# The first modulation vectors as VectorE sums, x^T last in halves, and the expert biases in one 128-partition tile

## The chip, the cores and the metric

The kernel runs on one core of a Trainium2 chip. The metric is the device time of one execution in microseconds (us), lower is better. Engines: PE does matmuls, DVE is VectorE, ACT is ScalarE, POOL is GpSimd, and SP here only issues DMAs. ACT issues DMAs of its own as well.

## The reference

One decoder layer on x (256 tokens by 1024) and a conditioning vector c (1024):

```python
mod = jax.nn.silu(c) @ w_ada + b_ada                  # 1024 x 6144
sh_a, sc_a, g_a, sh_f, sc_f, g_f = jnp.split(mod, 6)
h = x * (1.0 + sc_a) + sh_a
mix = hybrid_mixer(h, w_in, ret_norm_g, w_out, rel_bias)
x = layer_norm(DN_ALPHA * x + (1.0 + g_a) * mix, ln1_g, ln1_b)
h = x * (1.0 + sc_f) + sh_f
ff = moe(h, w_router, b_router, w_gate_up, b_gate_up, w_down, b_down)
x = layer_norm(DN_ALPHA * x + (1.0 + g_f) * ff, ln2_g, ln2_b)
```

The mixer multiplies h by w_in, feeds a top-64 sparse softmax attention with a relative bias and a retention branch, and projects the two with w_out. The mixture of experts picks 4 of 32 experts per token; each has 8 MB of gate and up weights, 4 MB of down weights, and bias rows b_gate_up and b_down.

## The kernel before, in words

Weights come on SP's queue as tiles of 128 x 2048 f32 (1 MiB) into a ring of six buffers (`rtile`, tag w); large named buffers (`spare`, tags x0 to x10) hold the rest. ACT's queue (`small`) carries small loads. A scheduler sets each engine's order from the dependences and its own cost estimates; `tc.issue_after` pins a few instructions behind others. Each engine executes its list strictly in order, and a DMA stands in the list of the engine that issues it, so a DMA that waits holds up what is behind it.

**Start.** `mod_step(0, k)` (L163, k = 0 to 7) loads eight tiles of w_ada, 128 input rows by the 2048 columns of sh_a and sc_a. PE multiplies each with silu(c) (cT, broadcast to 32 columns) into `pm` (L110 is the line of every matmul helper). xT, the transposed x, is loaded behind the sixth tile. Then follow in a row: copy of pm to SBUF (`modrow`, L172 on DVE and L173 on ACT), four PE transposes (`pmt`, L179), the sums with b_ada (`sc` L231, `sha` L232), and hh = xT * sc + sha in rounded fp32r, four blocks on ACT (L238) and four on DVE (L240). hl is what the rounding left (L243 to L245).

**Projections.** `split` cuts every weight tile into whi (ACT, L263) and wlo (DVE, or POOL for every fourth, L264). `proj_t` runs hh x whi, hl x whi and hh x wlo on PE. w_idx (544 columns) is the first tile projected, then twelve w_in tiles.

**Attention.** `softmax(s, r)`: POOL adds `bias` (a 1 MB tile of relative biases) to the scores (L415), PE makes logits pl, DVE adds (L420) and takes the maximum (L422), ACT exponentiates (L425), DVE takes reciprocals (L427) and scales (L429), PE transposes into pp (L433), ACT copies (L435). The last two calls, softmax(1,0) and softmax(1,2), run at 105 to 124 us; the value projection `pv` and the gate parts of the modulation stand among them on PE.

**Expert biases.** `bias_rows` loads b_gate_up three times over as 96 x 2048, b_down as 96 x 1024 (L510, ACT's queue), makes a bf16 copy (ACT, L512) and two correction terms (DVE, L514 and L515). raw_bias_gu takes the buffer of `bias` (tag nn) once POOL has read that for the last time.

**Experts.** Each expert's twelve 1 MiB tiles stream through the ring (SP, L775 and L783), PE multiplies them; the loads begin at 133 us, while the mixer still runs, as far as buffers are free.

Of the kernel before, what the change touches and what calls it, by code (L numbers as in the profile page):

```python
# [28 lines left out]
def layouts(inputs):  # L29
# [55 lines left out]
    dn = g["b_down"].reshape(2, 32, 512).transpose(1, 0, 2).reshape(32, 1024)  # L85
    out = {"head": head, "cst": cst, "hot": np.concatenate([hot, rel], 1),
# [7 lines left out]
def layer(ctx, tc, t, out):  # L94
# [41 lines left out]
    small(out=dec, in_=t["row"])  # L136
    ident_r = sb("ident_r", 128, 128, pool=keep, dt=F32R)
    V.tensor_copy(ident_r, ident)
    pick = sb("pick", 96, 32, pool=keep, dt=BF16)
    V.tensor_add(pick, ident[0:96, 0:32], ident[0:96, 32:64])  # L140
    V.tensor_add(pick, pick, ident[0:96, 64:96])
    ones = sb("ones", 128, 128, pool=keep)
    G.memset(ones, 1.0)
# [14 lines left out]
    def mod_step(part, k, w=None):  # L158
        if k == 0:
            mods[part] = ps("s", name="pm")  # L160
        pm = mods[part]
        w = rtile() if w is None else w
        load(out=w, in_=t["w_ada"][0, k * 128:(k + 1) * 128, part * 2048:(part + 1) * 2048])  # L163
        for j in range(4):
            mm(pm[32 * j:32 * j + 32], cT[:, k], w[:, j * 512:(j + 1) * 512], k == 0, k == 7)

    def mod_row(part):
        row = sb("modrow", 128, 512, pool=keep)
        if part:
            V.tensor_add(row, mods[part], b_ada[:, part - 1])  # L170
        else:
            V.tensor_copy(row[:, 0:256], mods[part][:, 0:256])  # L172
            first["mod"] = A.activation(row[:, 256:512], mods[part][:, 256:512], AF.Copy)  # L173
# [59 lines left out]
    sc1, sha = [v.rearrange("p a b -> p (a b)") for v in (sc1, sha)]
    hh = spare("hh", 0, F32R).rearrange("p (k t) -> p k t", k=8)
    hl = spare("hl", 1, F32R).rearrange("p (k t) -> p k t", k=8)
    for b in range(8):
        if b % 2 == 0:
            A.activation(hh[:, b], xT[:, b], AF.Identity, bias=sha[:, b:b + 1], scale=sc1[:, b:b + 1])  # L238
        else:
            first["h"] = V.tensor_scalar(hh[:, b], xT[:, b], sc1[:, b:b + 1], sha[:, b:b + 1], op0=OP.mult, op1=OP.add)  # L240
    for b in range(0, 8, 2):
        f2 = sb("hfull", 128, 2, 256, bufs=2, tag="zT")
        V.tensor_scalar(f2[:, 0], xT[:, b], sc1[:, b:b + 1], sha[:, b:b + 1], op0=OP.mult, op1=OP.add)  # L243
        A.activation(f2[:, 1], xT[:, b + 1], AF.Identity, bias=sha[:, b + 1:b + 2], scale=sc1[:, b + 1:b + 2])
        V.tensor_sub(hl[:, b:b + 2], f2, hh[:, b:b + 2].bitcast(F32))  # L245
# [8 lines left out]

    nsplit = [0]

    def split(w):
        i = nsplit[0]
        nsplit[0] += 1
        n = w.shape[1]  # L260
        hi = spare("whi", 2 + 2 * (i % 2), F32R)[:, 0:n]
        lo = spare("wlo", 3 + 2 * (i % 2), F32R)[:, 0:n]
        first["split"] = A.activation(hi, w, AF.Copy)  # L263
        (G if i % 4 == 3 and i < 13 else V).tensor_tensor(lo, w, hi.bitcast(F32), op=OP.subtract)  # L264
        return hi, lo
# [41 lines left out]
    w = rtile()[:, 0:544]  # L307
    load(out=w, in_=t["w_idx"])
    with tc.issue_after(first["mod"].ins), tc.issue_after(first["h"].ins):
        w = [d.rearrange("p (k c) -> p k c", k=8) for d in split(w)]  # L310
# [3 lines left out]
    with tc.issue_after(first["split"].ins):  # L314
        load_later()
# [10 lines left out]
    for b in range(2):  # L326
        A.activation(blocks(qiT[:, b]), back(pq[:, b]), AF.Copy)
# [180 lines left out]
    def bias_rows(name, n, **kw):  # L508
        raw = sb("raw_" + name, 96, n, 512, **kw)
        small(out=raw, in_=t[name].rearrange("p (h c) -> p h c", h=n))  # L510
        b = sb(name, 96, n, 512, pool=keep, dt=BF16)
        A.activation(b, raw, AF.Copy)  # L512
        for o in (64, 32):
            V.tensor_sub(raw[0:o], raw[0:o], b[0:o])  # L514
            V.tensor_copy(b[0:o], raw[0:o])  # L515
        return b
# [62 lines left out]
    split_wo(3)  # L579

# [566 lines left out]
```

## Time and profile before

| | |
|---|---|
| median of 3 runs | 1137.49 us (1134.46 to 1137.56) |
| profiled execution: time, span | 1137.54 us, 1135.9 us |
| mean granted clock of PE | 0.981 |
| busy: PE, DVE, ACT, POOL | 92%, 32%, 16%, 4% |
| moved from and to memory | 452 MB, mean 398 GB/s |
| chain that ended last, two largest parts | 57% DMA, 36% PE |

Busy shares are means over the span. The chain that ended last is followed back from the last instruction to whatever released it each time, so it says which resource the end hangs on. The stretches show the same per slice of time: PE's busy time, its granted clock (1.00 is 2.4 GHz, 0.50 is 1.2 GHz), and the rate of the DMAs.

### The profile page before, as it was taken

What the parts mean: (1) busy time and instruction counts of PE and PEld (TensorE: products, weight loads), DVE (VectorE), ACT (ScalarE), POOL (GpSimd) and SP (SyncE); (2) the same over time, 40 slices, a digit from 0 to 9 for tenths busy, and PEclk for the clock granted to TensorE, in tenths of its full rate; (3) what the DMA queues carried; (4) which work ended last, traced back from release to release, by engine and by line L of the source; (5) the groups of instructions that cost most, each with busy time, mean ns of one, the idle gap of its engine ahead of it and who ended that gap; (6) DMA issues with size and microseconds to landing.
All of it is one profiled execution on the core that took longest, in us unless ns stands there. A gap on an engine that the chain in (4) does not pass through costs nothing.

```text
span 1135.9 us, 12046 instructions
## 1 busy us (share of the span) xinstructions
PE 1044.3 (92%) x4939; PEld 440.9 (39%) x4939; DVE 360.4 (32%) x661; ACT 177.4 (16%) x292; POOL 49.4 (4%) x38
## 2 busy tenths in 40 slices
PE   7999999999999999999999899989988689999895
PEld 1776676344334333433333233323422233233232
DVE  0676786123122222221322122212221212212125
ACT  1534634101101000100110001000100001100001
POOL 0124110300000000000000000000000000000001
PEclk9899999999899999999999999999999889999998
DMA  9988995999999999999999999999999999999993
GB/s 381 364 320 303 382 385 226 369 421 421 420 422 420 422 420 422 420 422 421 422 421 420 421 421 422 421 422 420 421 421 421 421 419 421 421 421 421 421 416 139
DMA packets 65861, 451.99 MB, mean 398 GB/s; under 512 B 7380, under 2 KB 8573, under 8 KB 11817
## 3 DMA queue, kind: packets, MB, share of 16 engines
q1 hardware_dynamic: 63536, 447.52, 95.6%
q10 hardware_dynamic: 2266, 3.65, 1.0%
q8 instruction: 41, 0.67, 0.2%
q14 instruction: 18, 0.15, 0.0%
HBM read 450.05 MB, written 1.09 MB: 397 GB/s over the span
## 4 chain that ended last, share of the span: by engine, by line
DMA 57%; PE 36%; DVE 4%; ACT 1%; issue 1%; SPq 0%; ACTq 0%; DVEq 0%
DMA w<-in_w_gate_up 37%; DMA w<-in_w_down 19%; PE py L110 7%; PE pgate L110 7%; PE pup L110 6%; PE pm L110 3%; PE pr L110 2%; PE pv L110 2%; PE pz L110 2%; PE pg L110 1%; PE psc L110 1%; PE pb L110 1%; PE pq L110 1%; PE pact L879 1%; DVE wlo L264 1%
## 5 line engine op out<-in xcount | busy, mean ns | idle before, releaser
L110 PE MATMUL pgate<-w,xe 128*64 128x512 f32 x1024 | 341.4, 604 | 24.5 <-DMA w<-in_w_gate_up 24.4
L110 PE MATMUL pup<-w,xe 128*64 128x512 f32 x1024 | 347.4, 594 | 0.0
L110 PE MATMUL py<-w,aT 128*64 128x512 f32 (+1 forms) x1056 | 244.5, 592 | 10.2 <-DMA w<-in_w_down 8.4
L110 PEld LDWEIGHTS pup<-w,xe 128*64 128x64 f32 x1024 | 101.2, 137 | 148.5 <-issue 144.7
L110 PEld LDWEIGHTS pgate<-w,xe 128*64 128x64 f32 x1024 | 90.5, 136 | 173.4 <-issue 92.5
L851 DVE TENSOR_SCALAR sw_g<-pgate 128x512 f32<-128x512 f32 x32 | 22.1, 692 | 396.7 <-PE pgate L110 396.7
L110 PEld LDWEIGHTS py<-w,aT 128*64 128x64 f32 x1056 | 72.0, 137 | 134.3 <-issue 90.4
L897 DVE TENSOR_TENSOR y<-py,gf 64x512 f32<-64x512 f32 x62 | 42.7, 689 | 194.9 <-PE py L110 194.5
L852 ACT ACTIVATE act<-sw_g 128x512 f32<-128x512 f32 x32 | 20.1, 630 | 487.5 <-DVE sw_g L851 487.5
L924 DVE TENSOR_TENSOR acc<-acc,psc 128x512 f32<-128x512 f32 x60 | 38.6, 684 | 23.5 <-PE psc L110 23.5
L1076 POOL TENSOR_TENSOR acc<-acc,ln 128x512 f32<-128x512 f32 (+1 forms) x2 | 2.7, 1342 | 903.5 <-ACT acc L1075 903.5
L803 DVE TENSOR_SCALAR xe<-pg,ha,hb 128x128 f32<-128x128 f32 x64 | 25.7, 409 | 49.6 <-PE pg L110 36.4
L880 ACT ACTIVATE aT<-pact 128x512 f32<-128x512 f32 x32 | 19.1, 597 | 119.9 <-PE pact L879 119.9
L263 ACT ACTIVATE whi<-w 128x2048 fp32r<-128x2048 f32 (+1 forms) x17 | 31.3, 1840 | 34.9 <-DMA w<-lay_w_in 16.3
L804 ACT ACTIVATE xe<-pg,hb,ha 128x128 f32<-128x128 f32 x64 | 28.5, 457 | 47.6 <-DVE xe L803 47.6
L110 PE MATMUL pm<-w,cT 128*32 128x512 f32 x192 | 35.6, 677 | 0.0
L110 PE MATMUL psc<-yh,ohT 128*128 128x512 f32 x60 | 25.4, 464 | 10.9 <-ACT yh L911 7.8
L110 PE MATMUL pg<-oh,nh 128*128 128x256 f32 x128 | 34.8, 306 | 0.5 <-DVE oh L656 0.3
L911 ACT ACTIVATE yh<-y,gs 128x1024 fp32r<-128x1024 f32 x15 | 17.2, 1148 | 107.1 <-DVE y L897 107.1
L110 PEld LDWEIGHTS <-pick 96*64 96x64 bf16 x190 | 15.2, 109 | 47.0 <-issue 44.7
L110 PE MATMUL pg<-oh,nl 128*128 128x256 f32 x128 | 33.4, 293 | 0.0
L264 DVE TENSOR_TENSOR wlo<-w,whi 128x2048 fp32r<-128x2048 f32 (+1 forms) x14 | 30.4, 2172 | 6.4 <-ACT whi L263 6.4
(262 smaller groups left out, 857.1 us busy)
## 6 DMA issues: line engine op xcount, KB each, us to landing
w<-in_w_gate_up SPq DMA_DIRECT2D x256, 1024.0 KB, 19.8
w<-in_w_down SPq DMA_DIRECT2D x124, 1024.0 KB, 19.8
w<-in_w_ada SPq DMA_DIRECT2D x24, 1024.0 KB, 6.9
w<-lay_w_in SPq DMA_DIRECT2D x12, 1024.0 KB, 8.8
w<-lay_w_out SPq DMA_DIRECT2D x4, 1024.0 KB, 11.3
w<-in_w_down SPq DMA_DIRECT2D x7, 512.0 KB, 12.7
xT<-lay_xT SPq DMA_DIRECT2D x1, 1024.0 KB, 14.5
x<-in_x SPq DMA_DIRECT2D x2, 512.0 KB, 10.5
```

Of the source, the lines that this page charges most:

```text
L110: T.matmul(o, l, r, start=start, stop=stop)
L263: first["split"] = A.activation(hi, w, AF.Copy)
L264: (G if i % 4 == 3 and i < 13 else V).tensor_tensor(lo, w, hi.bitcast(F32), op=OP.subtract)
L803: return V.tensor_scalar(xes[h][:, i], src, ha[:, i:i + 1], hb[:, i:i + 1], op0=OP.mult, op1=OP.add)
L804: return A.activation(xes[h][:, i], src, AF.Identity, bias=hb[:, i:i + 1], scale=ha[:, i:i + 1])
L851: V.tensor_scalar(g, pg, 7.0, None, op0=OP.min)
L852: A.activation(s, g, AF.Sigmoid, scale=1.702)
L879: T.transpose(pa[:, 2 * i + j], act[:, 256 * i + j:256 * i + j + 255:2], ident)
L880: A.activation(aT, pa, AF.Copy)
L897: V.tensor_mul(y[o:o + CAP, c], py[64 * c:64 * c + 64], gf[64 * c:64 * c + 64, c * 512:(c + 1) * 512])
L911: A.activation(yh, y, AF.Copy, scale=gs)
L924: V.tensor_add(o, o, p_)
```

## The change

Four things are done.

1. c is loaded first, as a row; PE broadcasts it to all partitions with a row of ones (`pc`, L143), ACT takes silu into cB. The weights of sh_a and sc_a are laid out by output column (`ada_t`), and DVE multiplies each 128 x 1024 half tile by cB and sums it into one column of `mcol` (16 instructions, L168). PE's matmuls, the row copies and the transposes of this part are gone.
2. SP's order at the start is now c, six weight tiles, `row`, tiles 6 and 7 in halves with w_idx between, xT in two halves, then the w_in tiles. w_idx is split ahead of hh.
3. hl, cT, ident_r and pick are pinned behind hh; the copy f8 moves from DVE to ACT; the load of `bias` moves behind the copy of the indexer's queries (L355).
4. The expert biases become one 128 x 768 tile `btmp` in the buffer of `bias` (L539). DVE makes three bf16 parts (L541 casts, L543 subtractions), they are written to memory (L545) and read back as 96 x 3072 by three DMAs (L611).

```diff
+    crow = spare("crow", 5)[0:1, 0:1024]
+    load(out=crow, in_=t["c"])
...
+    cB = spare("cB", 4)[:, 0:1024]
+    for j in range(2):
+        pc = ps("s", name="pc")
+        pcs = T.matmul(pc, ones[0:1], crow[:, j * 512:(j + 1) * 512], start=True, stop=True)
+        cbs = A.activation(cB[:, j * 512:(j + 1) * 512], pc, AF.Silu)
...
+    def mod_sums(i, w, pieces=1):
+        n = 2048 // pieces
+        for p in range(pieces):
+            load(out=w[:, p * n:(p + 1) * n], in_=t["ada_t"][i, :, p * n:(p + 1) * n])
+        for b in range(2):
+            wb = w[:, b * 1024:(b + 1) * 1024]
+            first["sum"] = V.scalar_tensor_tensor(wb, wb, 1.0, cB, op0=OP.mult, op1=OP.mult,
+                                                  accum_out=mcol[:, 2 * i + b:2 * i + b + 1])
...
-        small(out=bias, in_=bass.AP(tensor=fap.tensor, offset=fap.offset, ap=[[1, 128], [384, H], [1, 256]]))
...
+    for i in range(8):
+        mod_sums(i, rtile() if i < 6 else spare("w", i - 6), 1 if i < 6 else 2)
+        if i == 0:
+            sums1 = first["sum"]
+        if i == 5:
+            load(out=dec, in_=t["row"])
+        if i == 6:
+            w_first = rtile()[:, 0:544]
+            load(out=w_first, in_=t["w_idx"])
+    for p in range(2):
+        load(out=xT[:, 4 * p:4 * p + 4], in_=t["xT"].rearrange("p (k t) -> p k t", k=8)[:, 4 * p:4 * p + 4])
...
-    for k in range(8):
-        mod_step(0, k, None if k < 6 else spare("w", k - 6))
-        if k == 5:
-            load(out=xT, in_=t["xT"].rearrange("p (k t) -> p k t", k=8))
-
-
-    ca = mod_cols(mod_row(0), 0, 4)
...
+    w_first = split(w_first)
+
+
+    sha, sc1 = sb("sha", 128, 8), sb("sc1", 128, 8)
+    V.scalar_tensor_tensor(sc1, mcol[:, 8:16], 1.0, b_sa[:, 8:16], op0=OP.add, op1=OP.add)
+    V.tensor_add(sha, mcol[:, 0:8], b_sa[:, 0:8])
...
+    with tc.issue_after(qis.ins):
+        small(out=bias, in_=bass.AP(tensor=fap.tensor, offset=fap.offset, ap=[[1, 128], [384, H], [1, 256]]))
...
-    b_gu = bias_rows("bias_gu", 4, pool=keep, tag="nn")
-    b_dn = bias_rows("bias_dn", 2, tag="k4a")
+    btmp = sb("btmp", 128, 2048, pool=keep, tag="nn")
+    raw, bpart = btmp[:, 0:768], btmp[:, 768:1920].bitcast(BF16).rearrange("p (o c) -> p o c", o=3)
+    small(out=raw, in_=t["biases"])
+    for o in range(3):
+        V.tensor_copy(bpart[:, o], raw)
+        if o < 2:
+            V.tensor_sub(raw, raw, bpart[:, o])
+    bd = dram.tile([3, 128, 768], BF16, name="bd")
+    small(out=bd.rearrange("o p c -> p o c"), in_=bpart)
+    b_all = sb("b_all", 96, 3072, pool=keep, dt=BF16)
...
+    with tc.issue_after(first["split"].ins):
+        for o in range(3):
+            small(out=b_all[32 * o:32 * o + 32].rearrange("r (u c) -> r u c", u=4),
+                  in_=bd[o].rearrange("(u r) c -> r u c", u=4))
```

The lines of the kernel shift with the change: L263 and L264 become L229 and L230, and the softmax's L415, L420, L422, L425, L427, L429, L433 and L435 become L443, L448, L450, L453, L455, L457, L461 and L463. Behind the names of the rows below stand `[waits ...]`: the engines or DMA lanes whose signal an instruction waits for.

The first place is DVE at the start. Before, the list up to hh was:

```order
L153 COPY cT<-sg 128x256
L172 COPY modrow<-pm 128x256
L231 SCALAR_TENSOR_TENSOR sc_177<-pmt,head 128x8
L232 TENSOR_TENSOR sha<-pmt,head 128x8
L240 TENSOR_SCALAR hh<-xT,sc_177,sha 128x256 x4
```

Now it begins with:

```order
L168 SCALAR_TENSOR_TENSOR w,mcol<-w,cB 128x1024 x8
L261 TENSOR_TENSOR sha<-mcol,head 128x8
L168 SCALAR_TENSOR_TENSOR w,mcol<-w,cB 128x1024 x6
L230 TENSOR_TENSOR wlo<-w,whi 128x544
L168 SCALAR_TENSOR_TENSOR w,mcol<-w,cB 128x1024 x2
L260 SCALAR_TENSOR_TENSOR sc_162<-mcol,head 128x8
L268 TENSOR_SCALAR hh<-xT,sc_162,sha 128x256 x4
```

The copy of the row and the sums with the transposed columns are replaced by sixteen products with sums, with the split of w_idx between the last of them.

The second place is ACT ahead of the exponentials (L425, now L453) of softmax(1,0). Before:

```order
L263 ACTIVATE whi<-w 128x2048 [waits DMAHW7_49,Pool_49]
L510 DMA raw_bias_dn<-lay_bias_dn 96x1024 [waits PE_49]
L425 ACTIVATE scr_69,sm<-scr_69,mx 128x256 [waits DVE_49,Activation_49]
L425 ACTIVATE scr_69,sm<-scr_69,mx 128x256
L425 ACTIVATE scr_69,sm<-scr_69,mx 128x256 [waits DVE_49,Activation_49]
L425 ACTIVATE scr_69,sm<-scr_69,mx 128x256
L263 ACTIVATE whi<-w 128x2048 [waits DMAHW2_49]
```

Now:

```order
L229 ACTIVATE whi<-w 128x2048 [waits DMAHW3_49,Pool_49]
L539 DMA btmp<-lay_biases 128x768 [waits DMAHW7_49,Pool_49]
L453 ACTIVATE scr_69,sm<-scr_69,mx 128x256 [waits DVE_49,Activation_49]
L453 ACTIVATE scr_69,sm<-scr_69,mx 128x256
L453 ACTIVATE scr_69,sm<-scr_69,mx 128x256 [waits DVE_49,Activation_49]
L453 ACTIVATE scr_69,sm<-scr_69,mx 128x256
L463 ACTIVATE scr_71<-pp 128x2x256 [waits PE_49]
```

The load of btmp, which waits for POOL's last read of `bias`, stands ahead of the exponentials; before, the load that waited for POOL (raw_bias_gu) stood behind them and behind the copies of pp, and the one here waited for PE.

The third place is DVE in softmax(1,0), whose scaling (L429, now L457) PE's transposes pp wait for. Before:

```order
L420 SCALAR_TENSOR_TENSOR scr_69<-pl,scr_69 128x512 [waits DVE_49,PE_49] x2
L422 TENSOR_REDUCE mx<-scr_69 128x2 [waits DVE_49] x2
L427 RECIPROCAL sm<-sm 128x2 [waits Activation_49]
L429 TENSOR_SCALAR scr_69<-scr_69,sm 128x256 [waits DVE_49]
L429 TENSOR_SCALAR scr_69<-scr_69,sm 128x256
L427 RECIPROCAL sm<-sm 128x2 [waits Activation_49]
L429 TENSOR_SCALAR scr_69<-scr_69,sm 128x256 [waits DVE_49]
L429 TENSOR_SCALAR scr_69<-scr_69,sm 128x256
```

Now:

```order
L448 SCALAR_TENSOR_TENSOR scr_69<-pl,scr_69 128x512 [waits DVE_49,PE_49] x2
L450 TENSOR_REDUCE mx<-scr_69 128x2 [waits DVE_49] x2
L230 TENSOR_TENSOR wlo<-w,whi 128x2048 [waits DMAHW3_49,Activation_49]
L455 RECIPROCAL sm<-sm 128x2 [waits Activation_49]
L541 CAST btmp<-btmp 128x768 [waits DMAHW7_49,Pool_49]
L457 TENSOR_SCALAR scr_69<-scr_69,sm 128x256 [waits DVE_49]
L457 TENSOR_SCALAR scr_69<-scr_69,sm 128x256
L455 RECIPROCAL sm<-sm 128x2 [waits Activation_49]
L543 TENSOR_TENSOR btmp<-btmp 128x768 [waits DVE_49]
L457 TENSOR_SCALAR scr_69<-scr_69,sm 128x256 [waits DVE_49]
L457 TENSOR_SCALAR scr_69<-scr_69,sm 128x256
```

The first cast of btmp, which waits for that load to land, stands between the reciprocal and the scaling; a wlo and a subtraction of the biases have come in as well.

## Rows read from the trace of the kernel before

**Rows 1.** page, part 4: shares of the chain that ended last, by engine
```profile
DMA 57%; PE 36%; DVE 4%; ACT 1%; issue 1%; SPq 0%; ACTq 0%; DVEq 0%
```

**Rows 2.** stretches: start:end us; length; busy PE, PEld, DVE, ACT, POOL; clock; DMA share; GB/s
```profile
10.00:20.00 10.00, 10.00 (x23) 2.57 (x25) 0.00 (x0) 2.13 (x5) 0.63 (x1) 1.00 1.01 422
30.00:32.00 2.00, 1.24 (x6) 0.80 (x6) 1.96 (x7) 1.93 (x4) 0.00 (x0) 0.77 1.02 426
32.00:34.00 2.00, 1.48 (x6) 0.61 (x5) 2.00 (x5) 2.00 (x4) 0.00 (x0) 0.50 0.97 401
130.00:140.00 10.00, 10.00 (x48) 7.10 (x46) 9.61 (x7) 4.95 (x3) 0.00 (x0) 1.00 1.00 415
170.00:180.00 10.00, 10.00 (x60) 8.60 (x59) 7.16 (x19) 3.24 (x5) 0.00 (x0) 1.00 0.19 75
180.00:190.00 10.00, 8.00 (x53) 7.18 (x52) 7.54 (x20) 2.04 (x3) 0.00 (x0) 0.83 0.89 360
210.00:220.00 10.00, 10.00 (x33) 3.47 (x34) 1.38 (x2) 1.19 (x2) 5.04 (x3) 0.90 0.69 269
```

**Rows 3.** waits of SP, 0 to 240 us: us in total, times, longest
```profile
SPq L775 <- PE pup L110: 20.5, 9, 9.8
```

**Rows 4.** chain that ended last within 0 to 62 us: start, us, what
```profile
18.57 9.83 PE pm L110 x58
...
29.88 0.17 DVE sha L232
...
30.07 2.07 ACT hh L238 x4
...
49.36 4.25 issue
```

**Rows 5.** DMA issues, 0 to 240 us: operation, KB each, median us to landing
```profile
raw_bias_gu<-lay_bias_gu ACTq DMA_DIRECT2D x1, 768.0 KB, 7.9
cst<-lay_cst ACTq DMA_DIRECT2D x1, 536.0 KB, 8.2
...
head<-lay_head ACTq DMA_DIRECT2D x1, 76.0 KB, 5.5
```

**Rows 6.** tile w, 0 to 12 us: issues (first and last start us) and landing times
```profile
L163 SPq DMA_DIRECT2D w<-in_w_ada x8: 328/420/792, 0.9 to 7.8; - x8
...
DMA to landing us min/median/max: 5.3/11.0/13.3
```

**Rows 7.** PE timeline: start, us, operation, idle before and releaser
```profile
16.50 2.07 PE L110 MATMUL ps_t<-scr,ones 1*128 1x512 f32 x2
...
113.41 0.60 PE L433 MATMUL pp<-head,scr 128*128 128x128 f32 x4
```

**Rows 8.** ACT timeline, the same columns
```profile
18.60 0.60 ACT L214 ACTIVATE scr<-ps_t 128x512 f32<-128x512 f32 x1 [3.47 <-PE ps_t L110]
```

**Rows 9.** DVE timeline, the same columns
```profile
32.02 0.72 DVE L264 TENSOR_TENSOR wlo<-w,whi 128x544 fp32r<-128x544 f32 x1
...
110.78 0.69 DVE L429 TENSOR_SCALAR scr<-scr,sm 128x256 f32<-128x256 f32 x2
...
138.70 2.27 DVE L264 TENSOR_TENSOR wlo<-w,whi 128x2048 fp32r<-128x2048 f32 x1
140.90 0.68 DVE L515 CAST bias_dn<-raw_bias_dn 32x1024 bf16<-32x1024 f32 x1
...
182.65 1.27 DVE L653 SCALAR_TENSOR_TENSOR nl<-acc,lsd,nh 128x1024 fp32r<-128x1024 f32 x1
183.83 0.20 DVE L627 BATCH_NORM_AGGREGATE lmv<-lst 128x2 f32<-128x12 f32 x1
...
195.41 0.08 DVE L714 DVE_READ_ACCUMULATOR gate<-gate,msk 128x1 f32 x1
```

**Rows 10.** POOL timeline, the same columns
```profile
48.89 4.64 POOL L264 TENSOR_TENSOR wlo<-w,whi 128x2048 fp32r<-128x2048 f32 x1 [6.06 <-ACT whi L263]
...
108.55 2.51 POOL L415 TENSOR_TENSOR scr<-bias,score 128x512 f32<-128x512 f32 x2
```

More of the change, by code (lines that the diff above doesn't have):

```diff
@@ L135, in layer @@
     dec = scr9[0:1]
[L136 to L143, printed above, removed]
     slots = sb("slots", 128, CAP, pool=keep)
@@ L168, in mod_row @@
         row = sb("modrow", 128, 512, pool=keep)
[L169 to L173, printed above, removed]
+        V.tensor_add(row, mods[part], b_ada[:, part - 1])
         return row
@@ L188, in layer @@
     pf = ps("t")
-    mm(pf[0:8, 0:384], hot[:, 384:392], hot[:, 0:384])
+    with tc.issue_after(pcs.ins):
+        mm(pf[0:8, 0:384], hot[:, 384:392], hot[:, 0:384])
     f8 = scr7[0:8, 1, 0:384]
-    V.tensor_copy(f8, pf[0:8, 0:384])
+    with tc.issue_after(cbs.ins):
+        A.activation(f8, pf[0:8, 0:384], AF.Copy)
     fd = dram.tile([8, 384], F32, name="fd")
@@ L199, in load_later, with split @@
         small(out=b_ada[0:128:32], in_=t["b_ada"])
-        small(out=bias, in_=bass.AP(tensor=fap.tensor, offset=fap.offset, ap=[[1, 128], [384, H], [1, 256]]))
         small(out=rows_[0:72], in_=t["rows"])
+        return fap
+    cst = sb("cst", 128, 1072)
+    below, acausal = cst[:, 0:128], cst[:, 128:256]
+    cos, sin = cst[:, 256:512], cst[:, 512:768]
+    lnc, w_rt, b_rt = cst[:, 768:784], cst[:, 784:1040].rearrange("p (k e) -> p k e", k=8), cst[0:1, 1040:1072]
+    rows_ = sb("rows_", 128, 512, pool=keep)
+    xT = spare("xT", 10).rearrange("p (k t) -> p k t", k=8)
+    nsplit = [0]
+    def split(w):
+        i = nsplit[0]
+        nsplit[0] += 1
+        n = w.shape[1]
+        hi = spare("whi", 2 + 2 * (i % 2), F32R)[:, 0:n]
+        lo = spare("wlo", 3 + 2 * (i % 2), F32R)[:, 0:n]
+        first["split"] = A.activation(hi, w, AF.Copy)
+        (G if i % 4 == 3 and i < 13 else V).tensor_tensor(lo, w, hi.bitcast(F32), op=OP.subtract)
+        return hi, lo
+    for i in range(8):
[9 more added lines that the diff above has]
+        load(out=xT[:, 4 * p:4 * p + 4], in_=t["xT"].rearrange("p (k t) -> p k t", k=8)[:, 4 * p:4 * p + 4])
     decay = scr8[:, 0:1024].rearrange("p (h c) -> p h c", h=4)
@@ L237, in layer @@
         if b % 2 == 0:
-            A.activation(hh[:, b], xT[:, b], AF.Identity, bias=sha[:, b:b + 1], scale=sc1[:, b:b + 1])
+            first["hA"] = A.activation(hh[:, b], xT[:, b], AF.Identity, bias=sha[:, b:b + 1], scale=sc1[:, b:b + 1])
         else:
[L240 to L245, printed above, removed]
+            first["hV"] = V.tensor_scalar(hh[:, b], xT[:, b], sc1[:, b:b + 1], sha[:, b:b + 1],
+                                          op0=OP.mult, op1=OP.add)
+    with tc.issue_after(first["hA"].ins), tc.issue_after(first["hV"].ins):
+        for b in range(0, 8, 2):
+            f2 = sb("hfull", 128, 2, 256, bufs=2, tag="zT")
+            V.tensor_scalar(f2[:, 0], xT[:, b], sc1[:, b:b + 1], sha[:, b:b + 1], op0=OP.mult, op1=OP.add)
+            A.activation(f2[:, 1], xT[:, b + 1], AF.Identity, bias=sha[:, b + 1:b + 2], scale=sc1[:, b + 1:b + 2])
+            V.tensor_sub(hl[:, b:b + 2], f2, hh[:, b:b + 2].bitcast(F32))
+    sg = sb("sg", 128, 8)
+    cT = sb("cT", 128, 8, 32)
+    with tc.issue_after(first["hA"].ins), tc.issue_after(first["hV"].ins):
+        A.activation(sg, c8, AF.Silu)
+        V.tensor_copy(cT, sg[:, :, None].to_broadcast([128, 8, 32]))
+        ident_r = sb("ident_r", 128, 128, pool=keep, dt=F32R)
+        V.tensor_copy(ident_r, ident)
+        pick = sb("pick", 96, 32, pool=keep, dt=BF16)
+        V.tensor_add(pick, ident[0:96, 0:32], ident[0:96, 32:64])
+        V.tensor_add(pick, pick, ident[0:96, 64:96])
     queue = [(p, k) for p in (1, 2) for k in range(8)]
@@ L252, in mod_next @@
         del queue[:n]
[L255 to L265, printed above, removed]
     ntile = [0]
@@ L304, in back @@
         return blocks(a)[:, :, ::-1]
[L307 to L310, printed above, removed]
+    w = [d.rearrange("p (k c) -> p k c", k=8) for d in w_first]
     pk = ps("g")
@@ L504, in layer @@
         V.tensor_mul(rn[:, s], rn[:, s], gr[:, s])
[L508 to L516, printed above, removed]
-    b_gu = bias_rows("bias_gu", 4, pool=keep, tag="nn")
-    b_dn = bias_rows("bias_dn", 2, tag="k4a")
+    btmp = sb("btmp", 128, 2048, pool=keep, tag="nn")
[8 more added lines that the diff above has]
+    b_all = sb("b_all", 96, 3072, pool=keep, dt=BF16)
+    b_gu = b_all[:, 0:2048].rearrange("p (g c) -> p g c", g=4)
+    b_dn = b_all[:, 2048:3072].rearrange("p (g c) -> p g c", g=2)
     acc = sb("acc", 128, 2, D, pool=keep, tag="nn")
```

30 lines of the change are left out of this document (10 added, 20 removed).

## The prediction

> **What bounds the kernel now.** I read the page's chain of waits first. More than half of it is DMA, a third is PE, and DVE and ACT have 5% together [rows 1]. The stretches then tell when each of the two bounds. From the first projection to about 170 us PE is busy all the time, while DMA is also nearly full (1.00 at 130 to 140 us). At 170 to 180 us PE is still full and DMA falls to a share of 0.19, and at 210 to 220 us it is at 0.69 with 269 GB/s [rows 2]. SP waits there for PE: its waits for `pup` before 240 us add up to 20.5 us [rows 3]. So the stream of expert weights is short of free buffers, and PE's chain of work through the mixer frees them. Behind that the stream is the bound to the end. The consequence is the rule that I use for everything below: a microsecond that PE's chain loses or gains before about 200 us moves the start of the last, stream-bound part by a microsecond, and with it the end.
>
> The start is a chain of its own. PE's last part of the modulation runs for 9.8 us up to 28.4, the copies, the transposes and sha take until 30.05, and the first hh starts at 30.07 [rows 4]. What the change does to the start is what it does to that 30.07; what it does later is what it does to PE.
>
> **The start, step by step.** c is the first load. The first weight tile, 1.05 MB, landed 5.3 us after its issue [rows 6]; at the 422 GB/s of this stretch [rows 2] its bytes take 2.5 us, and with some 0.2 us for its place in the queue 2.6 us are left that do not depend on size. With SP's first issue at 0.9 us [rows 6], c (4 KB) is there at 3.5 us. The upper end is the small load of `head`, 5.5 us [rows 5], with which c lands at 6.4 us. PE then broadcasts it in two matmuls of one row by 512 columns; the same shape took 2.07 us [rows 7], so 4.1 us, until 7.6 us. ACT's silu of the second half, like its 512-column pass of 0.60 us [rows 8], ends at 8.4 us with 0.2 us for the two hand-overs.
>
> Then DVE has sixteen products with sums over 128 x 1024. No row shows one. The nearest is a product and sum of three tensors of the same size, 1.27 us long, whose successor started 1.18 us after it, and the row that reads out an accumulator, 0.08 us [rows 9]. I take 1.18 + 0.08 = 1.26 us each, so 20.2 us. The split of w_idx stands among them (the first place in the section on the change) with 0.72 us [rows 9], and sha and sc1 with about 0.3 us. DVE reaches hh at 8.4 + 20.2 + 0.72 + 0.3 = 29.6 us, and with 0.2 us of handing over, 29.8. The DMAs alone would be done earlier: 9.86 MB come before xT's second half is complete (c, eight tiles, head, hot, row, w_idx and xT), 23.4 us at 422 GB/s, so 0.9 + 2.6 + 23.4 = 26.9 us. That is the lower bound, 27.1 us for hh. The upper bounds are sums at the full 1.27 + 0.08 us (+1.4) or c landing at 6.4 us (+2.9).
>
> So hh starts at 29.8 instead of 30.07, a gain of 0.3 us. Against it stands PE's clock. Before, PE worked without a break until 28.4 us, at a granted 1.00 [rows 2], and the first two microseconds of the projections still had 0.77. Now its matmuls of the modulation are gone, and it has only short work between about 8 and 29 us. Before, the clock fell to the lower level of 1.2 GHz after PE's short breaks from 28.4 us on: 0.50 at 32 to 34 us [rows 2]. I expect it at the lower level from the first matmul, which costs the (0.77 - 0.50) x 2 = 0.5 us that the first stretch had above that level, and the rise may come a little earlier or later. The start comes to **+0.4 us**, with the ends -3.0 and +2.9. The Trainium skill, page TensorE: Matmul & The Clock Gate, Part 1, says that an idle PE runs at half its clock and that only work brings the full one back; that speaks against a start that takes PE's work away. The rows agree with it, since 0.50 follows the breaks.
>
> f8 on ACT, the moved load of `row` and the pinned hl, cT, ident_r and pick are counted at nothing: DVE, ACT and SP have nothing due then that PE waits for before hh. If hl came later than PE's first eight matmuls of ps_g, each 0.1 us of that would show. In the top-k stage DVE stood from 49.36 us for 4.25 us, until POOL's wlo of 4.64 us from 48.89 was over [rows 4, 10]; the same pair exists again. I count no difference there, with 1 us either way.
>
> **The biases.** What is removed is two casts on ACT and eight operations on DVE, the last at 140.90 us [rows 9]. PE is full ahead of that [rows 2], and waits for none of them, so they are worth nothing.
>
> What is added stands in a worse place. On ACT the load of btmp now stands ahead of the exponentials of softmax(1,0), and it waits for POOL's last read of `bias` (second place). Before, those reads were two, from 108.55 us, and ended at 111.06 [rows 10]. DVE's first cast then waits for the landing, and the scaling of softmax(1,0), which PE's transposes pp need, is behind that cast (third place). Before, that scaling ran at 110.78 [rows 9], and PE came to pp at 113.41 us without any wait [rows 7].
>
> Now the load is issued at 111.1 us, or at 113.3 if the wlo that has come in on DVE beside POOL's reads, 2.27 us long [rows 9], runs first and POOL waits for it, as DVE waited for POOL at 49.36 us. Its 0.39 MB take 0.9 us at 422 GB/s. What lies above the bytes was 2.6 us for the first weight tile, 6.0 for raw_bias_gu (7.9 less 0.79 MB at that rate) and 6.9 for cst (8.2 less 0.55 MB) [rows 5, 6]. So it lands after 3.5 to 7.8 us; both upper rows are loads of ACT's queue beside the weight stream, but the one of 128 partitions here has fewer bytes ahead of it, and I take the middle, 5.7 us. The cast, at 768/1024 of 0.68 us, is 0.5 us, the first scaling 0.69 [rows 9]. pp can begin at 111.1 + 5.7 + 0.5 + 0.7 = 118.0 us, or at 120.2 with the later issue: PE waits 4.6 or 6.8 us. I take **5.5 us**; the ends are 2.4 (3.5 us, early issue) and 8.9 (7.8 us, late issue). The Trainium skill, page DMA: Bandwidth & Descriptors, section on the anatomy of one DMA, gives a fixed 2.0 us and the bytes at 436 GB/s; by that the load would land after 2.9 us and PE would wait 1.8 us. The rows of this queue are three times as long as that rule for their sizes, so the sum stays with the rows.
>
> Behind it two things follow. The rest of the two softmax calls has the subtractions and two more casts between its steps, each some 0.5 us on DVE, where PE's later pp of softmax(1,2) is due: **+0.5 us**. And PE's clock falls after such a break: the stretch 180 to 190 us, with 2.0 us idle, had 0.83, which is 1.7 us of work lost, and the two from 30 to 34 us lost 0.5 + 1.0 = 1.5 us [rows 2]. I take **+1.5 us**, with ends 0 and 3, where the lower level lasts on.
>
> The write of bd, its three loads back and 0.39 MB more of traffic lie behind the last split of w_out, ahead of the first expert; nothing of it is on the chain.
>
> **Sum.** 0.4 + 5.5 + 0.5 + 1.5 = 7.9 us. On the profiled execution's 1137.54 us this is **1145.4 us**; the median of the runs shown, 1137.49, is the same.
>
> **Rivals.**
>
> *A, the delay of PE is hidden behind the weight stream; not slower.* At 130 to 140 us DMA is as full as PE [rows 2]. If the stream there sets the pace of what comes next, and the split of a weight tile would have waited for it, PE loses 7.5 us at 113 us and regains it before 200. The time would be 1137.5 + 0.4 = 1138; with a start at the DMA's pace, 1134.5. The point that decides is the stretch 170 to 180 us: if DMA's share of 0.19 there fills up while PE's chain ends no later, A holds. Against it: PE is full in that stretch without waiting, so it has no slack in which to regain anything. Chance 0.12.
>
> *B, a good start and a quick load.* If the sums keep up with the DMA (-3.0 us) or the load lands near 3.5 us (stall 2.4 us, and little of the clock lost), the sum is between -3.0 + 2.4 + 0.5 = 0 and 0.4 + 2.4 + 0.5 + 0.8 = +4.1, so 1137.5 to 1141.6, say 1140. For it: the sums are only 1.26 us against the 1.24 us in which 0.52 MB come at 422 GB/s, so DVE's lag is the late beginning at 8.4 us. Chance 0.18.
>
> *C, the late end.* The issue waits for 113.3 us and the landing takes 7.8 us, or the clock stays low for longer: 0.4 + 8.9 + 0.5 + 1.5 = 11.3, so 1149; with a late c, 1151. For it: both loads of this queue with some hundred KB were at 7.9 and 8.2 us. Chance 0.15.
>
> *D, the change does not do what the list says.* If the cast's wait ended before PE's arrival, because POOL's last reads came much earlier, the biases would cost nothing and the time would be 1137.9. POOL's reads wait for buffers that DVE's L420 frees, and came at 108.55 us [rows 10], so I see no way to it. Chance 0.03.
>
> **How the numbers follow.** The forecast has 0.52; its own range is 1142 to 1148.5. A and D sit within a microsecond of the time before, B between there and 1141.6, C above 1148.5. The range that leaves out no more than 2 in 10 goes from 1137 to 1150.5: it takes in all of B, C but for its end, and half of A. A measurement of this kernel can tell 0.3%, or 3.4 us, from no change: faster is below 1134.1, slower above 1140.9. Faster needs A together with the start's lower end, or something that I have not seen: 0.07. Same has the rest of A and D, half of B and the edge of the forecast: 0.22. Slower has the rest: 0.71.
>
> **What would show it.** In the profile after: first hh at 29.8 us, sixteen sums of about 1.26 us each from 8.4 us, and a granted clock at the lower level for the first projections. At 111 us an ACT issue of btmp behind POOL's last read; a cast on DVE whose idle time ends on the DMA of btmp; PE idle for 4 to 7 us ahead of pp of softmax(1,0), ended by DVE's scaling, and a clock under 1.00 behind it. At 170 to 220 us the same dips of the DMA rate, some 8 us later. I am wrong if PE does not wait at pp, if hh starts before 28 or after 32 us, or if PE's delay at 125 us is not there any more at 215 us.

## The result and the profile after

The changed kernel takes 1144.7 us (median of 10 runs, 1141.74 to 1147.6) against 1137.53 us (10 runs, 1134.46 to 1142.8): ratio 1.0063, 95% interval [1.0048, 1.0079]. It is slower by 7.2 us, or 0.63%, which is clear of the 0.3% that the prediction set as its bound. Forecast were 1145.4 us, in a range of 1137 to 1150.5. The profiled execution after took 1145.46 us, its span 1143.7 us, 7.8 more than before.

First the stretches of the kernel after (columns as in [rows 2]), those that answer to the ones shown before and two that show the loss:

```profile
10.00:20.00 10.00, 1.05 (x3) 0.86 (x4) 9.79 (x18) 0.00 (x0) 0.00 (x0) 1.00 1.01 418
...
30.00:32.00 2.00, 1.30 (x4) 0.60 (x4) 2.00 (x5) 1.83 (x5) 0.00 (x0) 1.00 1.05 438
32.00:34.00 2.00, 1.67 (x7) 1.37 (x8) 1.68 (x5) 1.46 (x1) 0.00 (x0) 1.00 0.98 410
...
110.00:120.00 10.00, 1.95 (x7) 1.76 (x8) 3.00 (x9) 2.87 (x10) 0.00 (x0) 0.66 0.62 260
120.00:130.00 10.00, 10.00 (x52) 6.87 (x51) 7.46 (x14) 5.46 (x13) 0.00 (x0) 0.82 0.34 116
130.00:140.00 10.00, 10.00 (x52) 6.88 (x51) 2.70 (x1) 5.67 (x5) 4.60 (x1) 1.00 1.02 395
...
180.00:190.00 10.00, 8.99 (x59) 7.75 (x57) 7.31 (x21) 2.65 (x4) 0.00 (x0) 1.00 0.29 98
190.00:200.00 10.00, 9.00 (x56) 7.52 (x58) 7.92 (x24) 4.33 (x9) 0.00 (x0) 0.83 0.88 369
```

At 10 to 20 us PE is nearly empty and DVE full. At 110 to 120 us PE works for 1.95 us of ten, at a clock of 0.66, and still has only 0.82 in the next ten. DMA is down to a share of 0.34 there: its buffers are not freed, since SP waits 16.7 us in a row for PE's pm. The dip of DMA to 75 GB/s at 170 to 180 us [rows 2] has become 98 GB/s, one stretch later. In stretches of two microseconds the share of 0.03 and then 0.00 stands at 174 to 180 us before and at 182 to 188 us after, so the dip came 8 us later, as forecast.

PE's timeline after, at the first projections (ps_g and pq are products with w_idx and the first w_in tile), at the wait, at the next part of the modulation, and at the last wait of the mixer (pz is the product with w_out):

```profile
27.79 2.17 PE L113 MATMUL ps_g<-hh,whi 128*68 128x256 f32 x8 [3.35 <-ACT hh L266]
...
35.13 1.91 PE L113 MATMUL pq<-hh,whi 128*128 128x256 f32 x8
...
39.35 1.12 PE L113 MATMUL pq<-hh,whi 128*128 128x256 f32 x8
...
109.28 0.39 PE L113 MATMUL pv<-whi,hh 128*128 128x512 f32 x1
118.05 1.11 PE L461 MATMUL pp<-head,scr 128*128 128x128 f32 x4 [8.38 <-DVE scr L457]
118.82 0.77 PE L113 MATMUL pv<-whi,hl 128*128 128x512 f32 x1
119.39 0.63 PE L113 MATMUL pv<-whi,hh 128*128 128x512 f32 x1
...
124.59 1.92 PE L113 MATMUL pm<-w,cT 128*32 128x512 f32 x16
...
174.75 0.50 PE L113 MATMUL pz<-wlo,ch 128*128 128x512 f32 x1 [1.08 <-DVE wlo L230]
```

The same places before, as far as [rows 7] does not show them:

```profile
30.72 2.17 PE L110 MATMUL ps_g<-hh,whi 128*68 128x256 f32 x8 [0.96 <-ACT hh L238]
...
40.93 1.12 PE L110 MATMUL pq<-hh,whi 128*128 128x256 f32 x8
...
117.35 1.92 PE L110 MATMUL pm<-w,cT 128*32 128x512 f32 x16
...
167.55 0.50 PE L110 MATMUL pz<-wlo,ch 128*128 128x512 f32 x1 [1.07 <-DVE wlo L264]
```

PE has done its work ahead of pp at 109.67 us, 3.74 us earlier than before (113.41, [rows 7]). Then it stands for 8.38 us, and the pv behind that take 0.63 us instead of 0.39. What releases it is on DVE:

```profile
16.39 1.22 DVE L168 SCALAR_TENSOR_TENSOR w<-w,cB 128x1024 f32<-128x1024 f32 x1
17.54 0.08 DVE L168 DVE_READ_ACCUMULATOR w<-w,cB 128x1 f32 x1
17.54 1.22 DVE L168 SCALAR_TENSOR_TENSOR w<-w,cB 128x1024 f32<-128x1024 f32 x1
...
106.28 2.32 DVE L230 TENSOR_TENSOR wlo<-w,whi 128x2048 fp32r<-128x2048 f32 x1
111.37 0.17 DVE L455 RECIPROCAL sm<-sm 128x2 f32<-128x2 f32 x1 [2.77 <-ACT scr L453]
117.17 0.56 DVE L541 CAST btmp<-btmp 128x768 bf16<-128x768 f32 x1 [5.64 <-DMA btmp<-lay_biases]
117.65 0.61 DVE L457 TENSOR_SCALAR scr<-scr,sm 128x256 f32<-128x256 f32 x2
```

The reciprocal is ready at 111.5 us; the scaling that PE needs begins at 117.65, because the cast ahead of it waits for the DMA of btmp. ACT's and POOL's timelines give the issue, and the DMA list the landing:

```profile
109.78 0.36 ACTq L539 DMA_DIRECT2D btmp<-lay_biases  x1
```

```profile
105.16 4.59 POOL L443 TENSOR_TENSOR scr<-bias,score 128x512 f32<-128x512 f32 x2
```

```profile
btmp<-lay_biases ACTq DMA_DIRECT2D x1, 384.0 KB, 7.3
```

POOL's last read of `bias` ends at 109.75 us, the load is issued at 109.78 and lands 7.3 us later.

The loss adds up on PE. It came to pp 3.74 us earlier, waited 8.38 us, and needed 124.59 - 118.05 = 6.54 us from pp to the end of this weight tile, against 117.35 - 113.41 = 3.94 us before for the same instructions, in a slightly different order and without a wait, so 2.60 us went to the lower clock. That is -3.74 + 8.38 + 2.60 = +7.24 us. The last wait of the mixer on PE, for the wlo of the last w_out tile, ends at 174.75 us instead of 167.55, +7.20, and the span is 7.8 us longer. Nothing was regained on the way. SP's list shows the same delay where the stream of expert weights begins, before and after, +7.98 us:

```profile
133.73 47.48 SPq L775 DMA_DIRECT2D w<-in_w_gate_up  x16
```

```profile
141.71 0.33 SPq L808 DMA_DIRECT2D w<-in_w_gate_up  x1
```

### The profile page after: what moved, and what is told of

It reads as the page before. It is cut to its first block, busy times and chain, and to the rows that moved or that the text cites. A ratio compares the mean times of both kernels' runs of the same rounds, so it can differ in the third digit from the quotient of the medians.

```text
span 1143.7 us, 11958 instructions
## 1 busy us (share of the span) xinstructions
PE 1031.7 (90%) x4875; PEld 441.0 (39%) x4875; DVE 370.3 (32%) x688; ACT 175.7 (15%) x292; POOL 50.6 (4%) x38
## 5 line engine op out<-in xcount | busy, mean ns | idle before, releaser
L113 PE MATMUL py<-w,aT 128*64 128x512 f32 (+1 forms) x1056 | 241.9, 586 | 11.2 <-DMA w<-in_w_down 9.5
L230 DVE TENSOR_TENSOR wlo<-w,whi 128x2048 fp32r<-128x2048 f32 (+1 forms) x14 | 31.6, 2256 | 16.5 <-ACT whi L229 16.5
L229 ACT ACTIVATE whi<-w 128x2048 fp32r<-128x2048 f32 (+1 forms) x17 | 31.2, 1837 | 30.6 <-DMA w<-lay_w_in 9.8
L113 PEld LDWEIGHTS pg<-oh,nh 128*128 128x128 f32 x128 | 25.1, 196 | 12.1 <-issue 6.4
```

## The experiments

Theory W: the wait behind the cast of btmp and the clock behind it are the loss, and the start by itself is a gain. Against it stood S (the start's lead is given back anyway) and X (the bytes and instructions of the new bias code cost, not their place). One measure is used for all profiles below: the end of the last wait for wlo in the mixer, the first `pz<-wlo` that waits on PE (167.55 before, 174.75 after). All times of runs are medians, with the ratio to the kernel before on the same chip. That kernel had medians of 1136.6 to 1137.7 us on these chips, so small differences between runs are read from the ratios.

### The old biases put back into the changed kernel

```diff
-    btmp = sb("btmp", 128, 2048, pool=keep, tag="nn")
...
+    b_gu = bias_rows("bias_gu", 4, pool=keep, tag="nn")
+    b_dn = bias_rows("bias_dn", 2, tag="k4a")
```

> The changed kernel with the old preparation of the biases (96-partition tiles, ACT casts, DVE corrections) put back. Theory W (PE's wait at pp behind the cast of btmp, and the low clock after it, are the whole loss; the start by itself gains what PE is ahead at 109 us, 3.7 us): about 1133.8 us, no PE wait over 1 us at pp of softmax(1,0). Rival S (the lead of the start is given back before the experts, whatever the biases do): 1137.5. Rival X (the traffic and the extra instructions of the new biases cost, not their place): also 1133.8.

1137.92 us, ratio 1.0015 [1.0000, 1.0029]. The wait at pp is gone (0.70 us), and pp begins at 109.05 us, 4.36 us ahead of before. So the loss of the change goes with the new bias code. But the gain that W and X forecast (1133.8) is missing, as S said: the last wait ends at 167.58 us, as before. Where the lead went, on DVE and then on PE:

```profile
125.08 5.62 DVE L544 CAST bias_gu<-raw_bias_gu 64x2048 bf16<-64x2048 f32 x1
...
134.57 1.21 DVE L544 CAST bias_gu<-raw_bias_gu 32x2048 bf16<-32x2048 f32 x1
135.71 2.27 DVE L230 TENSOR_TENSOR wlo<-w,whi 128x2048 fp32r<-128x2048 f32 x1
```

```profile
129.68 2.09 PE L113 MATMUL pv<-wlo,hh 128*128 128x512 f32 x8 [0.72 <-POOL wlo L230]
...
138.04 2.11 PE L113 MATMUL pv<-wlo,hh 128*128 128x512 f32 x8 [1.42 <-DVE wlo L230]
```

```profile
129.66 1.92 ACT L229 ACTIVATE whi<-w 128x2048 fp32r<-128x2048 f32 x1 [2.44 <-POOL wlo L230]
```

ACT's whi is done at 131.6 us, but DVE is in the bias corrections until 135.7, and PE waits for the wlo. So it seems that the bias work, which hid behind PE before, is in PE's way once PE comes four microseconds earlier; two runs further down try this.

### The new biases put into the kernel before

```diff
-    b_gu = bias_rows("bias_gu", 4, pool=keep, tag="nn")
-    b_dn = bias_rows("bias_dn", 2, tag="k4a")
...
+    btmp = sb("btmp", 128, 2048, pool=keep, tag="nn")
```

> The kernel before with only the new preparation of the biases. In its compiled order the cast stands behind the first scaling of softmax(1,0) and ahead of the second. W: the load is issued when POOL's last read ends (111.1), lands after 7.3 us, the second pp can begin near 120.8 where PE came at 114.3: a wait of 6.5 us and 2.5 us of low clock, 1146.5. X: the same size, but without one long PE wait.

1146.46 us, ratio 1.0084 [1.0065, 1.0103]; the last wait ends at 173.92 us, +6.37. PE's wait is 4.81 us at the second pp of softmax(1,0), where 6.5 were expected. So the loss appears without the new start, with one long wait of PE, as W said. That the time meets the forecast of 1146.5 is in part luck: the median rose by 9.9 us on this chip, the last wait by 6.37 only, and the other 3.5 us were not located.

### The same bias work, pinned behind the softmax

```diff
-    small(out=raw, in_=t["biases"])
-    for o in range(3):
-        V.tensor_copy(bpart[:, o], raw)
...
+    with tc.issue_after(first["exp"].ins), tc.issue_after(first["sm"].ins):
+        small(out=raw, in_=t["biases"])
+        for o in range(3):
+            V.tensor_copy(bpart[:, o], raw)
...
```

> The changed kernel with the load of btmp pinned behind the exponentials and its casts behind the scalings of softmax(1,2); the same bytes and instructions. W: no PE wait at pp, 1133.8 as with the old biases. X: 1144, since nothing of the work is gone. S: 1137.5.

1134.03 us, ratio 0.9980 [0.9963, 0.9996]: some 10 us under the changed kernel, with every byte and instruction of the change. X falls. Against the kernel before it is 0.2%, and the interval just leaves out 1. DVE in this run:

```profile
107.53 1.96 DVE L457 TENSOR_SCALAR scr<-scr,sm 128x256 f32<-128x256 f32 x4
...
117.06 0.56 DVE L542 CAST btmp<-btmp 128x768 bf16<-128x768 f32 x1 [1.06 <-DMA btmp<-lay_biases]
117.66 0.96 DVE L544 TENSOR_TENSOR btmp<-btmp 128x768 f32<-128x768 f32 x1
```

The scaling runs at 107.53, the cast at 117.06 where nobody waits for what is behind it. PE waits 0.70 us at pp, and the last wait ends at 164.70 us, 2.85 us ahead of before.

### The raw biases in a buffer of their own

```diff
-    btmp = sb("btmp", 128, 2048, pool=keep, tag="nn")
-    raw, bpart = btmp[:, 0:768], btmp[:, 768:1920].bitcast(BF16).rearrange("p (o c) -> p o c", o=3)
+    raw = sb("btmp", 128, 768)
+    bpart = sb("bpart", 128, 2048, pool=keep, tag="nn")[:, 0:1152].bitcast(BF16).rearrange("p (o c) -> p o c", o=3)
```

> The changed kernel with the raw biases in a 3 KB buffer of their own, so that the load need not wait for POOL's last read; only the bf16 parts go into the buffer of bias, and the cast keeps its place ahead of the scaling. W: the cast waits for POOL's read alone (about 109.8), scaling near 110.9, PE waits some 1.5 us instead of 8.4 and keeps its clock: 1135.5. X: 1144. If the cast itself (0.56 us) rather than its wait for the load were the cost, 1144 as well.

1135.83 us, ratio 0.9993 [0.9979, 1.0007]. The cast stands where it stood in the change, and costs little:

```profile
109.92 0.56 DVE L541 CAST bpart<-btmp 128x768 bf16<-128x768 f32 x1 [1.04 <-POOL scr L443]
```

PE waits 0.97 us at pp and the last wait ends at 165.12 us. The load now is issued at 2.0 us, among the first weights, and the first projection begins at 28.72 us instead of 27.75 in the run before; that is about the time of its bytes (0.9 us at 422 GB/s). So what cost was the wait for the landing, not the cast.

### PE kept at work in the wait

```diff
...
+                d = T.matmul(junk[0:2], sm, cst[:, 256:768], start=True, stop=True)
+                for _ in range(6):
+                    with tc.issue_after(d.ins):
+                        d = T.matmul(junk, ones, cst[:, 256:768], start=True, stop=True)
+                pins.enter_context(tc.issue_after(d.ins))
...
```

> The changed kernel with seven additional matmuls, whose results nothing reads (one of two columns that waits for the first reciprocal, six of 128 x 512), between PE's value projection and pp of softmax(1,0), and pp pinned behind them; the wait for btmp stays. Its pp still cannot begin before about 118 us. Theory C (PE's long wait also costs some 2.5 us of low clock behind it): the pv matmuls behind pp take 0.39 to 0.40 us as before the change, not 0.63, and the time is some 1.5 us under the changed kernel's, 1143, the three pv that now stand behind the wait taken off. Rival N (the clock behind the wait costs nothing that is not regained): 1144.7 to 1145.5.

1151.2 us, ratio 1.0124 [1.0101, 1.0147]: both forecasts of the time miss, by more than 5 us. PE's timeline of this run:

```profile
118.43 0.70 PE L470 MATMUL pp<-head,scr 128*128 128x128 f32 x4 [1.48 <-DVE scr L457]
119.88 0.70 PE L470 MATMUL pp<-head,scr 128*128 128x128 f32 x4 [0.75 <-DVE scr L457]
120.34 0.48 PE L113 MATMUL pv<-whi,hh 128*128 128x512 f32 x1
120.66 0.39 PE L113 MATMUL pv<-whi,hl 128*128 128x512 f32 x1
...
127.93 0.63 PE L470 MATMUL pp<-head,scr 128*128 128x128 f32 x4 [2.71 <-DVE scr L457]
```

The pv behind the wait take 0.39 us, as theory C said: the 0.63 of the change was the clock. But pinning pp moved DVE's list as well; all casts now stand ahead of softmax(1,2), and PE waits 2.71 us more there. What the clock is worth in the end was not measured by itself; the 2.60 us come from the two timelines.

### PE kept at work at the start

```diff
+        for _ in range(8):
+            mm(junk, ones, cB[:, 0:512])
...
+        for _ in range(4):
+            mm(junk, ones, cB[:, 0:512])
```

> The run with the biases late plus twelve additional matmuls at the start (128 x 512, nothing reads them), eight behind the product with hot and four behind the last one with dec, so that PE works while DVE sums. Theory C2 (the first projections ran at the lower clock because PE was idle; they took 1.9 us for eight instead of 1.1): 2 us less than the run with late biases, 1132. Rival D2 (the first projections wait for hl, whi and wlo in any case, or the clock falls again in the gap before hh): 1134, or later by up to 1 us if the last four delay the first projection.

1134.52 us, ratio 0.9973 [0.9960, 0.9985]. The first pq now take 1.13 us for eight at 34.51 us instead of 1.75 at 35.10, and the last wait ends at 163.77 us, 0.9 us ahead of the run with late biases. So the clock of the first projections came from PE's idle start, as C2 said, but the gain is about half of its 2 us. The last four matmuls delayed the first projection (28.54 against 27.75). Runs of one kernel spread over up to 8 us, so 0.9 us shows in the profile and not in the times.

### The split of w_idx behind hh

```diff
-    w_first = split(w_first)
...
+    A.activation(hi, w_first, AF.Copy)
...
+    with tc.issue_after(first["hV"].ins):
+        V.tensor_tensor(lo, w_first, hi.bitcast(F32), op=OP.subtract)
...
```

> The run with the biases late, and the subtraction that splits w_idx pinned behind hh instead of between the sums. If DVE's sums set the start, hh begins 0.8 us earlier (26.3 instead of 27.1) and the time is up to 0.8 us lower, 1133.3; if the landing of xT sets it, hh stays at 27.1 and the time at 1134.

1136.58 us, ratio 0.9994 [0.9978, 1.0010]; the runs lie from 1131.42 to 1139.21, and the times show no gain. By the profile hh begins at 26.57 us instead of 27.10, and the last wait ends at 164.12 us, 0.6 us ahead. In the run with late biases DVE had already waited 0.16 us for the second half of xT: sums and DMA end nearly together there.

### The old biases without correction terms

```diff
-        for o in (64, 32):
-            V.tensor_sub(raw[0:o], raw[0:o], b[0:o])
-            V.tensor_copy(b[0:o], raw[0:o])
```

> The run with the old biases, with their two correction terms left out: the eight operations of DVE on them (14 us) are gone, loads and ACT casts stay. Theory B (with the start's lead PE arrives early enough to be held up by those eight operations, which stand ahead of the wlo that it needs): the waits of pv for wlo (0.7 and 1.4 us) go, and the time falls by 2 to 3 us, to 1135 to 1136. Rival S (the lead is given back by something else, the order of PE's own list or the buffers): 1137.9, as with the terms.

1134.63 us, ratio 0.9980 [0.9964, 0.9996], a little below theory B's 1135 to 1136. The profile agrees only in part: PE's wait for DVE is gone, but one of 1.20 us for ACT's whi has come in its place (behind the casts, which wait for their load until 121.02 us), and the last wait ends at 166.60 us, only 1.0 us earlier.

### No bias work at all

```diff
-        raw = sb("raw_" + name, 96, n, 512, **kw)
-        small(out=raw, in_=t[name].rearrange("p (h c) -> p h c", h=n))
...
-        A.activation(b, raw, AF.Copy)
+        G.memset(b, 0.0)
```

> The new start with the old code of the biases, of which nothing is left but two tiles that POOL sets to zero: no load, no ACT cast, no DVE term, so the biases of the experts are left out of the result. Theory B2 (the whole of the old bias work, DVE's terms and ACT's casts that wait for their load, took the start's lead between 109 and 140 us): PE's last wait for wlo ends near 164.7 as in the run with the biases late, the first bias matmul of the experts starts near 184 to 185, and the time is 1133.5 to 1135. Rival S (something else takes the lead): 1137.

1135.2 us, ratio 0.9981 [0.9966, 0.9996]. The last wait ends at 165.25 us, 2.3 us earlier than with the old biases. The first bias matmul begins at 187.34 us, later than forecast, for a reason of its own (last section). So the old bias work, DVE's and ACT's together, took 2.3 us of the 4.36 us that PE was ahead at pp. The rest is lost whatever the biases do: with the biases late PE is 4.65 us ahead at pp (108.76 against 113.41 us) and 2.85 at the last wait. At least part of it goes to two matmuls of the modulation that stand alone there at 115.70 us, for 1.05 us.

### Three steps together

The late biases, the split behind hh, and eleven matmuls at the start; the edits are those above, with one line different:

```diff
-        for _ in range(4):
+        for _ in range(3):
             mm(junk, ones, cB[:, 0:512])
```

> The biases late, the split of w_idx behind hh and eleven additional matmuls at the start together. Each of the two additions brought the first bias matmul of the experts forward by 0.6 to 0.9 us, to 183.4 and 183.1; if they add, it starts near 182.5 and the time is 1132 to 1133; if they overlap, 183 and 1134.

1134.77 us, ratio 0.9973 [0.9961, 0.9986], the last wait ends at 164.01 us. They don't add. The first bias matmul, at 186.10 us, is late for the same reason as in the run before.

## Why the prediction was right, point by point

**The time, right by terms that were off in opposite directions.** The sum was +7.9 us; the profile has +7.8, and the median +7.2. That they meet so closely is luck: PE's lead was 4.1 us better than the start's term (-3.74 against +0.4), the wait 2.9 us worse, the clock 1.1 us worse, and the later waits of 0.5 us did not come. The cause was the one that was forecast.

**The rule.** The prediction had a microsecond of PE's chain before 200 us pass to the end. The changes of the last wait against before were +7.20 (after), +6.37 (new biases only), -2.85 (late), -2.43 (own buffer), +12.8 (PE kept at work, 180.36); the profiled executions differ from the 1137.54 us of before by +7.9, +8.3, -3.6, -2.3 and +13.6. With the old biases it is less exact (+0.03 and +3.5): 1.0 us of that lies in the stretch of the last section, the rest was not located. In the other five runs the two numbers differ by 0.2 to 2.0 us. So single executions show the rule within 2 us for the 6 to 13 us lost here, and cannot show it for one microsecond. Rival A, that the stream hides the delay, did not hold: neither the last wait nor the first load of the experts regained anything.

**The start: forecast +0.4 us; this step failed.** hh begins at 27.14 us, not 29.8, 2.9 us earlier than before. That is within the ends of the term, but below the 28 us under which the prediction called itself wrong. Two terms were too large. c was there by 2.46 us, when PE began its broadcast, not at 3.5, and the first sum began at 6.88 us instead of 8.4. And the sums followed each other every 1.15 us, not 1.26: the row that reads out the accumulator begins with the next sum. The clock was right in kind, but its term of 0.5 us was too small. Eight matmuls of pq took 1.91 us at 35.13 us, and the full rate (1.12) came at 38.4 us; before, it came at about 38 us too (granted clock 0.53 at 36 to 38 us, 1.00 at 38 to 40). So PE was 2.93 us ahead at the first projection (27.79 against 30.72) and 1.58 us ahead at the second pq (39.35 against 40.93), with the same products between: 1.35 us were lost, 0.27 of them to longer waits for hl. The reading of 0.77 and 0.50 did not hold in its place, since the first eight ps_g took 2.17 us in both kernels.

**Another gain that was not seen.** Most of PE's lead at pp is not the start's. PE's busy time with the gate modulation ahead of that pp fell. By line, before and after:

```profile
L110 PE MATMUL pm<-w,cT 128*32 128x512 f32 x88 | 16.9, 601 | 0.0
```

```profile
L113 PE MATMUL pm<-w,cT 128*32 128x512 f32 x88 | 13.8, 599 | 0.0
```

The same 88 matmuls take 3.1 us less. The timeline shows where: fewer of them stand alone among others in the compiled order. One weight tile's sixteen, before and after:

```profile
94.28 1.90 PE L110 MATMUL pm<-w,cT 128*32 128x512 f32 x10
...
96.58 1.05 PE L110 MATMUL pm<-w,cT 128*32 128x512 f32 x4
...
97.83 1.05 PE L110 MATMUL pm<-w,cT 128*32 128x512 f32 x2
```

```profile
93.36 1.92 PE L113 MATMUL pm<-w,cT 128*32 128x512 f32 x16
```

In three pieces they take 4.00 us, in one 1.92; the next tile's go from two pieces of 2.96 us to one of 1.92. When this begins PE is only 0.92 us ahead (93.36 against 94.28), and at pp it is 3.74. So the new start brought some 0.9 us to this place and the compiled order some 2.8. The order was not tried by itself.

**The biases: the place, the chain of waits and their order right, the sizes too small.** The wait was 8.38 us, not 5.5. The landing took 7.3 us, near the upper end of 7.8, where the middle of 5.7 was chosen. The issue came at 109.78 us, not at 111.1 to 113.3: POOL's reads began earlier with PE, and took 4.59 us instead of 2.51 beside the wlo that has come in on DVE (2.32 us from 106.28 us). The prediction had seen this delay as its case of the late issue. In all pp began at 118.05 us, 0.9 us earlier than in the sum (113.41 + 5.5). But PE came 3.74 us earlier, and the whole of that went into the wait: 5.5 - 0.9 + 3.74 = 8.4. The Trainium skill, page DMA: Bandwidth & Descriptors, section on the anatomy of one DMA, gives its fixed 2.0 us and 436 GB/s for DMAs that GpSimd issues; carried over to this load of ACT's queue, an estimate, that is 2.9 us. The trace says 7.3, so the measurement decides. By that estimate the three rows of [rows 5] are 2.1 to 2.5 times too long, not three times as the prediction says. The 0.5 us for later waits did not occur.

**The clock behind the wait: forecast +1.5 us, measured 2.60.** The size was too small, within its ends of 0 and 3; that it is the clock, the run with PE kept at work shows by the 0.39 us of its pv.

**"Worth nothing".** The removed casts and corrections were rightly costed at nothing as long as PE stood where it stood before. With the new start they cost 2.3 to 2.9 us at the last wait (167.58 us with the old biases, 165.25 without bias work, 164.70 with the new ones late). The cover that the prediction named, PE full at 130 us, was the cover of the old start.

## What to carry to other kernels

When a step is moved to where its cost seems to vanish, look at what stands behind it on its engine: half a microsecond of cast was harmless, but it carried a wait for a load into the chain of the softmax. Of a lead, ask first where it came from: here most of it was the compiled order of other matmuls and not the earlier start. A gain at the start is worth nothing until the next wait that it meets has been looked at; here the lead was either spent in front of pp or taken in part by work that had been free. Read the compiled order for each instruction that waits for a DMA, and pin it behind the last instruction that the critical engine needs, as the run with the biases late did.

## What the runs showed of the hardware that was not expected

**A short wait can or can not cost the clock.** From the last wait to the first bias matmul of the experts the work is the same in all kernels, yet it took 19.3, some 20.8 or some 22 us. PE's last router products are the place where it begins to differ, in the run with late biases, in the kernel after, and in the run without bias work:

```profile
180.68 1.08 PE L113 MATMUL pr<-w_ha,zT 128*128 128x32 f32 x8 [0.74 <-ACT zT L651]
```

```profile
190.72 1.08 PE L113 MATMUL pr<-w_ha,zT 128*128 128x32 f32 x8 [0.75 <-ACT zT L650]
```

```profile
181.22 1.92 PE L113 MATMUL pr<-w_ha,zT 128*128 128x32 f32 x8 [0.75 <-ACT zT L640]
```

Behind the same two waits (0.97 us, then 0.74 or 0.75) the eight products take 1.08 or 1.92 us. The granted clock of 180 to 190 us was 1.00 with the biases late and 0.66 without bias work. In the kernel after it fell only behind these products, to 0.83 at 190 to 200 us. So single profiles differ by 1.5 to 2.8 us there, whatever was changed, which is why the last wait is the better measure.

**The granted clock of a stretch did not always follow the matmuls.** In the kernel after the stretches from 30 to 38 us show 1.00, as at 32 to 34 us above, while the same matmuls took 1.91 us that took 1.12 a little later. The durations tell the level there, 1.2 GHz, behind a stretch of 10 to 20 us in which PE had worked for 1.05 us. The Trainium skill, page TensorE: Matmul & The Clock Gate, Part 1, says that an idle PE is throttled and that activity releases the throttle; the durations agree with it, the granted clock shown does not.

**A pass of POOL held up a cast of DVE until it was over.** The cast at 125.08 us in the run with the old biases took 5.62 us, against 1.21 for one of the same width. It ended at 130.70 us, 1.08 us behind the end of this pass of POOL:

```profile
124.54 5.08 POOL L230 TENSOR_TENSOR wlo<-w,whi 128x2048 fp32r<-128x2048 f32 x1 [15.70 <-ACT whi L229]
```

Not every operation is held up: before the change, two reductions of DVE at 108.48 us, beside POOL's pass from 108.55 us [rows 10], took 1.27 us, as they did at 115.61 us without one. The Trainium skill, page SBUF — State Buffer, section Who interferes with whom, has a pair of ports that the two share and that belongs, for some operations of DVE, casts among them, to whichever came first for the whole instruction; these rows agree.
